# Products of identity and key lengths on VectorE, and the bonus sum behind the value products

## The chip, the cores and the metric

The kernel runs on one core of a Trainium2 chip. The metric is device time in microseconds from start to end of one execution of the program; the median over several executions is given. Engines are named as in the profile: PE is TensorE (matmuls; PEld its weight loads), DVE is VectorE, ACT is ScalarE, POOL is GpSimd, SP is SyncE, which issues most of the loads.

## The reference

One layer of a streaming encoder on x of 1 x 2048 x 1024 float32: a chunk-banded attention and an RWKV-7 recurrence side by side, a gated merge, and a feed-forward block. What matters here is the recurrence, with 8 heads of 64 channels:

```python
kk = heads(k * k_k)
kk = kk / jnp.maximum(jnp.sqrt(jnp.sum(kk * kk, axis=-1, keepdims=True)), 1e-12)
k = k * (1.0 + (a - 1.0) * k_a)
...
def step(state, inp):
    r_t, w_t, k_t, v_t, aa_t, bb_t = inp
    sa = jnp.einsum('bhij,bhj->bhi', state, aa_t)
    state = (state * w_t[:, :, None, :] + sa[..., None] * bb_t[:, :, None, :]
             + v_t[..., None] * k_t[:, :, None, :])
    y = jnp.einsum('bhij,bhj->bhi', state, r_t)
    return state, y

xs = tuple(jnp.moveaxis(t, 1, 0) for t in (r_h, w_h, k_h, v_h, -kk, kk * a_h))
...
bonus = jnp.sum(r_h * k_h * r_k.astype(jnp.float32), axis=-1, keepdims=True) * v_h
out = (yn + bonus) * heads(g)
```

## The kernel before

**Tiling and stages.** The 2048 positions are handled in four groups of 512 (`G`). For each group come the recurrence (`phase_rwkv`), the attention (`phase_attention`) and the merge (`phase_merge`); the feed-forward block follows for halves of the sequence. Dense products with the input weights run throughout: a float32 operand is split into a high and a low part, and three matmuls of 128x512 replace one (`mm3`, L83); ACT makes the high part of a weight block (L74), DVE the low one (L75).

**The recurrence.** A group has four pairs of heads, p = 0 to 3, handled as two batches of two; the first pair of a batch is the even one (p = 0 or 2), the second the odd one (p = 1 or 3). A group is cut into 8 chunks of 64 positions, and the recurrence inside a chunk is replaced by matrix products with the inverse of a triangular matrix. For each pair `rwkv_pre` makes everything that doesn't depend on the state: it mixes r, k and v (L353), computes decays (E, Ei), sums the squares of the keys (ps_ss, L441) and, on DVE, their reciprocals n2t (L443, L444); POOL spreads these with four small copies (L451) into n2, the key lengths by chunk and head of the pair (the profile leaves numbers out of names: n). Then come, in the order of the text:

- mN (L454), two products of 128x512, one for each head of the pair: the triangular mask mI, which holds for all chunks, times n2, both operands broadcast. Its only reader is L549, at the end of the preamble.
- AR and BK, scaled rows of keys and of r (L468 to L484).
- the bonus row: r times r_k times the key tk (L487, DVE), the sum over a head by a matmul with a block matrix of ones (ps_bonus, L489, PE), times v (L490, DVE), stored in `bvd[p]` by a DMA on POOL's queue (L491). `rwkv_post` reads it back (bv, L714) when the pair's recurrence is done.
- the value products: v times a centring matrix (ps_v, L498, PE), four ACT copies into SV (L502, L503).
- BK transposed on PE in two halves (ps_bk, L513), each multiplied by n2 on DVE into BR (L517).
- the products of BK and AR (ps_A, L533, PE), in two halves of two buffers each, and from these on DVE NA (L542), the rest of AR (L548) and the rest of BR (L549, with mN).

When both pairs of a batch are through, `rwkv_inverse` computes the triangular inverses of all their chunks in 31 steps of two small DVE instructions (L566, L572), with three block transpositions around them (L557, L575, L577); `rwkv_blocks` starts with matmuls of its result X1 (ps_t, L596). `rwkv_trans` and `rwkv_chunk` follow. Batch 1's preambles are interwoven with batch 0's recurrence: at each call of `between()` a list (`GATES`, `STEPS`) says how many gate products or recurrence steps stand at that place in the text.

**What sets the order.** Each engine works through one queue in a fixed order. The order is not that of the text: when the program is built, a scheduler plays it through with estimated durations, and each engine takes, of what is ready by that estimate, what stands first in the text. Dense matmuls of a later gate so fill places where PE would wait. On the chip the order stays as planned, and each instruction waits for its own inputs. Tiles of one tag share buffers in turn: all the PSUM results of the preamble (ps_ss, ps_bonus, ps_v, ps_bk, ps_A) and of the two following functions use tag `a` of pool `pa` with two buffers; mN has one buffer.

Of the kernel before, what the change touches and what calls it, by code (L numbers as in the profile page):

```python
# [8 lines left out]
F32 = mybir.dt.float32  # L9
# [3 lines left out]
ALU = mybir.AluOpType  # L13
# [4 lines left out]
P = 128  # L18
# [5 lines left out]
G = 512  # L24
GT = G // P
C = 64
NC = G // C
# [25 lines left out]
class Block:  # L53
# [342 lines left out]
    def rwkv_pre(self, g, p, rp, NA, between=lambda: None):  # L396
        nc = self.nc
# [3 lines left out]
        r = self.tmp("r")  # L401
# [12 lines left out]
        v = self.tmp("v")  # L414
# [31 lines left out]
        n2 = rp.tile([P, NC, 2], F32, tag="n2", name="n2")  # L446
        nc.gpsimd.memset(n2, 1.0)
        n2v = n2.rearrange("p (t h) e -> p h t e", h=2)
        for par in range(2):
            for h in range(2):  # L450
                nc.gpsimd.tensor_copy(n2v[par * C : par * C + C, h, :, par], n2t[h * C : h * C + C, :, par])  # L451
        mN = self.tp.tile([P, 2, NC, C], F32, tag="mN", bufs=1, name="mN")
        for par in range(2):
            nc.gpsimd.tensor_tensor(  # L454
                mN[:, par],
                self.mI[:, None, :].to_broadcast((P, NC, C)),
                n2[:, :, par, None].to_broadcast((P, NC, C)),
                ALU.mult,
            )
        between()  # L460

        AR = rp.tile([P, NC, 3, C], F32, tag="AR", name="AR")
# [22 lines left out]
        between()  # L485

        nc.vector.scalar_tensor_tensor(r, r, self.rk[:, col], tk, op0=ALU.mult, op1=ALU.mult)  # L487
        psb = self.pa.tile([P, G], F32, tag="a", name="ps_bonus")
        nc.tensor.matmul(psb, self.bones, r, start=True, stop=True)  # L489
        nc.vector.tensor_tensor(r, psb, v, ALU.mult)  # L490
        nc.gpsimd.dma_start(self.bvd[p], r)  # L491

        between()

        SV = rp.tile([P, NC, 2, C], F32, tag="SV", name="SV")
# [4 lines left out]
        for h in range(2):  # L500
            src = psv[h * C : h * C + C]
            nc.scalar.copy(SVv[C:P, h, :, 0], src[:, :, 0:C])  # L502
            nc.scalar.copy(SVv[0:C, h, :, 1], src[:, :, C:P])  # L503
        R["SV"] = SV

        between()

# [1087 lines left out]
```

## Time and profile before

| what | us |
|---|---|
| median of 3 runs | 3343.01 (3342.64 to 3346.67) |
| the profiled execution's own time | 3342.12 |
| its span in the profile | 3340.3 |

The granted clock of TensorE is 0.992 in the profiled execution. The DMA queues moved 478.42 MB, a mean of 143 GB/s. The span is what lies between the first and the last instruction that the profile shows; the execution's own time also holds what lies around it. In the profile's rows a group of instructions reads: line, engine, operation, written tile <- read tiles, partitions x elements, count | busy time, mean of one in ns | idle time of the engine just before them and what ended it. In a row of a timeline the first two numbers are start and duration in us, and the bracket at the end is the engine's idle time before it and its releaser. The waits view gives for each pair of waiter and releaser the total in us, how many times, and the longest.

The mix of the first low-rank columns (L352 on lw), with which a group's recurrence begins, starts at 35.0 us in the first group and at 1536.4 in the fourth; the last transpose of a post-processing (L704) starts at 1808.0.

### The profile page before, as it was taken

The numbers are of one execution on the slowest core, as the hardware profiler recorded it, in microseconds if no ns is written. First come the engines' busy times: TensorE is split into PE (matmuls) and PEld (weight loads), VectorE is DVE, ScalarE is ACT, GpSimd is POOL, SyncE is SP. The second block draws the span as 40 slices with busy tenths as digits, with TensorE's granted clock in tenths as the row PEclk, the third lists the DMA queues.
The fourth block names the chain that finished last, engine by engine and source line by source line (L and its number), as shares of the span: only waits on it lengthen the run. The fifth ranks groups of instructions, "written<-read, shape, count | busy, mean of one in ns | idle before, by whom it ended". The sixth has DMA issues, their size and how long they took to land. (4 is left out here: it accounts for less than half of the span.)

```text
span 3340.3 us, 49351 instructions
## 1 busy us (share of the span) xinstructions
PE 3247.1 (97%) x19089; PEld 2609.9 (78%) x19089; DVE 2282.6 (68%) x3806; ACT 1462.3 (44%) x2331; POOL 391.8 (12%) x732
## 2 busy tenths in 40 slices
PE   7999999999999999999999999999999999999998
PEld 6777787777778777777777777888888878888886
DVE  6774656765665775565774675876877777766778
ACT  4434634445644444644434644333331254554432
POOL 2210002111012110012210000111200011100002
PEclk9999999999999999999999999999999999999999
DMA  5224243125263225354224266434756364444443
GB/s 157 80 89 146 98 145 120 61 89 188 84 239 126 67 92 174 101 209 142 80 89 146 85 225 222 133 116 140 272 172 202 108 242 170 170 165 154 152 151 126
DMA packets 164945, 478.42 MB, mean 143 GB/s; under 512 B 17436, under 2 KB 34016, under 8 KB 162024
## 3 DMA queue, kind: packets, MB, share of 16 engines
q1 hardware_dynamic: 110004, 364.07, 32.8%
q0 software_dynamic: 18688, 63.98, 5.0%
q10 hardware_dynamic: 36020, 47.23, 3.9%
q8 instruction: 151, 2.47, 0.3%
q14 instruction: 82, 0.67, 0.1%
HBM read 355.64 MB, written 122.71 MB: 143 GB/s over the span
## 5 line engine op out<-in xcount | busy, mean ns | idle before, releaser
L83 PE MATMUL psd<-hh,whi 128*128 128x512 f32 x1344 | 542.6, 404 | 2.3 <-DVE QA L835 2.3
L83 PE MATMUL psd<-hl,whi 128*128 128x512 f32 x1344 | 539.4, 401 | 0.0
L83 PE MATMUL psd<-hh,wlo 128*128 128x512 f32 x1344 | 536.8, 399 | 0.0
L74 ACT CAST whi<-wraw 128x1024 fp32r<-128x1024 f32 x232 | 243.6, 1050 | 537.3 <-PE psd L83 423.7
L83 PE MATMUL ps_dn<-fop 128*128 128x512 f32 x1920 | 440.6, 391 | 3.0 <-DVE u L1291 2.4
L75 DVE TENSOR_TENSOR wlo<-wraw,whi 128x1024 fp32r<-128x1024 f32 x232 | 283.1, 1220 | 214.4 <-ACT whi L74 192.1
L83 PEld LDWEIGHTS ps_dn<-fop 128*128 128x128 f32 x1920 | 359.9, 188 | 79.5 <-DVE u L1291 3.4
L83 PEld LDWEIGHTS psd<-hh,whi 128*128 128x128 f32 x1344 | 256.1, 191 | 57.5 <-issue 3.4
L83 PEld LDWEIGHTS psd<-hh,wlo 128*128 128x128 f32 x1344 | 255.7, 190 | 54.0 <-issue 3.5
L83 PEld LDWEIGHTS psd<-hl,whi 128*128 128x128 f32 x1344 | 255.6, 190 | 50.9 <-issue 2.1
L83 PE MATMUL ps_dn<-fop,fop 128*128 128x512 f32 x1008 | 228.6, 389 | 0.0
L83 PEld LDWEIGHTS ps_dn<-fop,fop 128*128 128x128 f32 x1008 | 189.2, 188 | 39.3
L1291 DVE TENSOR_TENSOR u<-u,ps_dn 128x512 f32<-128x512 f32 x240 | 160.7, 683 | 54.9 <-PE ps_dn L83 54.4
L895 DVE CUSTOM_DVE_ANT_0 sc<-bias,ps_s 128x640 f32<-128x640 f32 (+4 forms) x128 | 94.1, 735 | 54.9 <-PE ps_s L889 44.0
L74 ACT CAST fop<-wdraw 128x1024 fp32r<-128x1024 f32 x40 | 41.9, 1047 | 192.0 <-DVE u L1291 88.7
L900 ACT ACTIVATE sc<-sc,mn 128x640 f32<-128x640 f32 (+4 forms) x128 | 97.8, 764 | 35.4 <-DVE mn L895 30.1
L74 ACT CAST s12h<-s 128x1024 fp32r<-128x1024 f32 x32 | 33.7, 1054 | 168.9 <-PE ps_u L83 168.8
L1019 PE MATMUL ps_o<-whi,mh 128*128 128x512 f32 x256 | 102.4, 400 | 2.2 <-ACT o L1025 2.2
L1019 PE MATMUL ps_o<-wlo,mh 128*128 128x512 f32 x256 | 102.5, 400 | 0.6 <-DVE wlo L75 0.6
L83 PE MATMUL ps_p<-yh,whi 128*128 128x512 f32 x256 | 102.2, 399 | 0.4 <-DVE th L985 0.4
L83 PE MATMUL ps_p<-yh,wlo 128*128 128x512 f32 x256 | 102.0, 398 | 0.0
L1019 PE MATMUL ps_o<-whi,ml 128*128 128x512 f32 x256 | 101.7, 397 | 0.0
(378 smaller groups left out, 6750.6 us busy)
## 6 DMA issues: line engine op xcount, KB each, us to landing
wraw<-in_w_in_dram SPq DMA_DIRECT2D x168, 512.0 KB, 3.6
wraw<-in_w_up_dram SPq DMA_DIRECT2D x80, 512.0 KB, 4.6
ar<-sd SPq DMA_DIRECT2D x21, 1024.0 KB, 4.8
wdraw<-in_w_down_dram SPq DMA_DIRECT2D x40, 512.0 KB, 4.2
araw<-ad SPq DMA_DIRECT2D x40, 512.0 KB, 4.4
gd<-gate ACTq DMA_DIRECT2D x64, 256.0 KB, 2.3
wraw<-in_w_out_dram SPq DMA_DIRECT2D x32, 512.0 KB, 3.6
ad<-r POOLq DMA_DIRECT2D x64, 256.0 KB, 2.4
```

The lines of the kernel that those rows point to most:

```text
L74: self.nc.scalar.copy(hi, src)
L75: self.nc.vector.tensor_tensor(lo, src, hi.bitcast(F32), ALU.subtract)
L83: mm = nc.tensor.matmul(ps, l, r, start=start and n == 0, stop=stop and n == last).ins
L895: nc.vector.tensor_tensor_reduce(sc[:, 0:n], bias[:, s0:640], pss[:, c0 : c0 + n], 1.0, 3.0e38, ALU.add, ALU.min, mn,)
L900: nc.scalar.activation(sc[:, 0:n], sc[:, 0:n], AF.Exp, scale=-1.0, bias=mn, accum_out=sm)
L1019: nc.tensor.matmul(ps[t], l[:, k, ts], r[:, k % 2], start=k == 0 and j == 0, stop=k == KB - 1 and j == 2)
L1291: nc.vector.tensor_tensor(u[t][:, ns], u[t][:, ns], ps, ALU.add)
```

## The change

Two blocks of `rwkv_pre` move. The two mN products leave POOL, where they stood behind the copies of n2, and stand on DVE behind the bonus row L487. The bonus matmul, its product with v and its DMA move behind the value products and the ACT copies, with the `between()` that stood after them now in front of the value products.

```diff
@@ -449,14 +449,6 @@
         for par in range(2):
             for h in range(2):
                 nc.gpsimd.tensor_copy(n2v[par * C : par * C + C, h, :, par], n2t[h * C : h * C + C, :, par])
-        mN = self.tp.tile([P, 2, NC, C], F32, tag="mN", bufs=1, name="mN")
-        for par in range(2):
-            nc.gpsimd.tensor_tensor(
-                mN[:, par],
-                self.mI[:, None, :].to_broadcast((P, NC, C)),
-                n2[:, :, par, None].to_broadcast((P, NC, C)),
-                ALU.mult,
-            )
         between()
 
         AR = rp.tile([P, NC, 3, C], F32, tag="AR", name="AR")
@@ -485,11 +477,14 @@
         between()
 
         nc.vector.scalar_tensor_tensor(r, r, self.rk[:, col], tk, op0=ALU.mult, op1=ALU.mult)
-        psb = self.pa.tile([P, G], F32, tag="a", name="ps_bonus")
-        nc.tensor.matmul(psb, self.bones, r, start=True, stop=True)
-        nc.vector.tensor_tensor(r, psb, v, ALU.mult)
-        nc.gpsimd.dma_start(self.bvd[p], r)
-
+        mN = self.tp.tile([P, 2, NC, C], F32, tag="mN", bufs=1, name="mN")
+        for par in range(2):
+            nc.vector.tensor_tensor(
+                mN[:, par],
+                self.mI[:, None, :].to_broadcast((P, NC, C)),
+                n2[:, :, par, None].to_broadcast((P, NC, C)),
+                ALU.mult,
+            )
         between()
 
         SV = rp.tile([P, NC, 2, C], F32, tag="SV", name="SV")
@@ -502,6 +497,11 @@
             nc.scalar.copy(SVv[C:P, h, :, 0], src[:, :, 0:C])
             nc.scalar.copy(SVv[0:C, h, :, 1], src[:, :, C:P])
         R["SV"] = SV
+
+        psb = self.pa.tile([P, G], F32, tag="a", name="ps_bonus")
+        nc.tensor.matmul(psb, self.bones, r, start=True, stop=True)
+        nc.vector.tensor_tensor(r, psb, v, ALU.mult)
+        nc.gpsimd.dma_start(self.bvd[p], r)
 
         between()
 
```

## The prediction

> **What bounds the kernel now.** I read the page first: its span and its busy times.
>
> ```profile
> span 3340.3 us, 49351 instructions
> ...
> PE 3247.1 (97%) x19089; PEld 2609.9 (78%) x19089; DVE 2282.6 (68%) x3806; ACT 1462.3 (44%) x2331; POOL 391.8 (12%) x732
> ```
>
> TensorE (PE) is busy in all but 3340.3 - 3247.1 = 93.2 us, so an edit that leaves its matmuls alone can only win or lose within its waits. Next the waits of PE, two rows of which touch the change:
>
> ```profile
> PE ps_t L596 <- DVE X L575: 26.6, 8, 3.8
> ...
> PE ps_bonus L489 <- DVE r L487: 8.1, 8, 1.2
> ```
>
> A preamble (rwkv_pre) runs 16 times, for pairs p = 0 to 3 in each of four groups. PE waits for the bonus row in 8 of them, and 8 times (two batches, four groups) for the end of the triangular inverse on VectorE. Together 34.7 us, over a third of all that PE idles. The order of time says which preambles. First pair 1 of the first group, from the timeline (columns: start, duration, engine, line, operation):
>
> ```profile
> 90.08 0.75 DVE L353 SCALAR_TENSOR_TENSOR v<-pr,cst,v 128x512 f32<-128x512 f32 x1
> ...
> 93.73 0.68 DVE L484 TENSOR_TENSOR BK<-tk,Ei 64x512 f32<-64x512 f32 x1
> 95.21 2.99 POOL L454 TENSOR_TENSOR mN<-mI,n 128x512 f32<-128x512 f32 x2
> 95.76 1.54 DVE L484 TENSOR_TENSOR BK<-tk,Ei 64x512 f32<-64x512 f32 x1
> 97.19 0.39 PE L83 MATMUL psd<-hh,whi 128*128 128x512 f32 x1
> 97.31 1.44 DVE L487 SCALAR_TENSOR_TENSOR r<-r,cst,tk 128x512 f32<-128x512 f32 x1
> 98.81 1.13 PE L489 MATMUL ps_bonus<-r,bones 128*128 128x512 f32 x2 [1.23 <-DVE r L487]
> ...
> 102.07 0.69 DVE L517 TENSOR_TENSOR BR<-ps_bk,n 128x512 f32<-128x512 f32 x1 [0.98 <-PE ps_bk L513]
> 103.11 0.69 DVE L517 TENSOR_TENSOR BR<-ps_bk,n 128x512 f32<-128x512 f32 x1 [0.36 <-PE ps_bk L513]
> 104.85 0.71 DVE L542 TENSOR_TENSOR NA<-ps_A,n 32x256 f32<-32x256 f32 x2 [1.04 <-PE ps_A L533]
> ...
> 143.85 1.20 PE L596 MATMUL ps_t<-X,NA 32*32 32x32 f32 x64 [2.83 <-DVE X L575]
> ```
>
> While GpSimd (POOL) makes the two products mN, the same L484 that took 0.68 us at 93.73 takes 1.54, and L487 takes 1.44 (a pair 0 row below shows 0.75). The stretch is 0.86 + 0.69 = 1.55 us, and PE waits 1.23 for r. That it is a habit and not an accident, the group rows say:
>
> ```profile
> L454 POOL TENSOR_TENSOR mN<-mI,n 128x512 f32<-128x512 f32 x32 | 43.9, 1388 | 1.3
> ...
> L484 DVE TENSOR_TENSOR BK<-tk,Ei 64x512 f32<-64x512 f32 x32 | 28.7, 896 | 0.0
> ...
> L487 DVE SCALAR_TENSOR_TENSOR r<-r,cst,tk 128x512 f32<-128x512 f32 x16 | 17.5, 1097 | 0.2
> ```
>
> (896 - 680) ns x 32 = 6.9 us and (1097 - 750) ns x 16 = 5.6 us, together 12.5: eight times 1.55. So the odd pairs (1 and 3) are stretched, the even ones not. After the bonus VectorE has hardly a gap up to the inverse's end; the stage view, taken between these moments, says so (columns: window, length, then busy time and count of PE, PEld, DVE, ACT, POOL):
>
> ```profile
> 105.00:144.00 39.00, 36.17 (x172) 29.20 (x173) 36.92 (x97) 16.18 (x24) 5.62 (x10) 1.00 0.27 85
> ...
> 206.50:245.00 38.50, 34.66 (x189) 27.77 (x188) 34.24 (x96) 13.64 (x20) 6.09 (x7) 1.00 0.33 117
> ```
>
> DVE is busy 36.92 of 39.00 us before pair 1's inverse ends and 34.24 of 38.50 before pair 3's. **So what bounds PE here is VectorE's path from the odd preamble to X (L575)**, not the bonus wait by itself. Pair 3 has the same shape:
>
> ```profile
> 197.06 1.54 DVE L484 TENSOR_TENSOR BK<-tk,Ei 64x512 f32<-64x512 f32 x1
> 198.62 1.44 DVE L487 SCALAR_TENSOR_TENSOR r<-r,cst,tk 128x512 f32<-128x512 f32 x1
> ...
> 200.12 1.12 PE L489 MATMUL ps_bonus<-r,bones 128*128 128x512 f32 x2 [0.80 <-DVE r L487]
> ...
> 203.47 0.52 DVE L679 SCALAR_TENSOR_TENSOR ST<-ps_st,gC,S 128x64 f32<-128x64 f32 x2 [0.91 <-PE ps_st L676]
> 204.25 0.69 DVE L517 TENSOR_TENSOR BR<-ps_bk,n 128x512 f32<-128x512 f32 x1 [0.26 <-PE ps_bk L513]
> ...
> 206.57 0.71 DVE L542 TENSOR_TENSOR NA<-ps_A,n 32x256 f32<-32x256 f32 x2 [0.65 <-PE ps_A L533]
> ...
> 244.93 1.83 PE L596 MATMUL ps_t<-X,NA 32*32 32x32 f32 x64 [3.84 <-DVE X L575]
> ```
>
> **The change, part by part.**
>
> *Products off GpSimd.* 32 instructions, 43.9 us of POOL, vanish. POOL is 12% busy and its own time is worth nothing; what counts is the 1.55 us of stretch in each odd preamble, 12.4 us in all, on VectorE's path to r and to X.
>
> *Products on VectorE.* The trace has no VectorE product of two stretched-out (broadcast) operands in SBUF. Neighbours:
>
> ```profile
> L1192 DVE TENSOR_TENSOR r<-r 128x512 f32<-128x512 f32 x64 | 43.8, 685 | 2.8 <-ACT r L1190 2.4
> ...
> L517 DVE TENSOR_TENSOR BR<-ps_bk,n 128x512 f32<-128x512 f32 x32 | 22.1, 690 | 15.4 <-PE ps_bk L513 15.1
> ...
> L421 DVE TENSOR_SCALAR tw<-tw 128x512 f32<-128x512 f32 x16 | 6.7, 421 | 0.0
> ```
>
> Same size and operation cost 685 to 690, one of them with the same key lengths n broadcast. The lower bound is 421 (one tensor input), the upper 1388, what GpSimd needs. I take 685: 1.37 us a preamble, 21.9 in all. In an odd preamble it lies on the path: 1.37 - 1.55 = -0.18. In an even one VectorE waits on others anyway:
>
> ```profile
> 59.66 0.75 DVE L487 SCALAR_TENSOR_TENSOR r<-r,cst,tk 128x512 f32<-128x512 f32 x1
> ...
> 63.15 0.69 DVE L517 TENSOR_TENSOR BR<-ps_bk,n 128x512 f32<-128x512 f32 x1 [0.82 <-PE ps_bk L513]
> 64.77 0.69 DVE L517 TENSOR_TENSOR BR<-ps_bk,n 128x512 f32<-128x512 f32 x1 [0.93 <-PE ps_bk L513]
> ...
> 92.72 2.41 POOL L451 COPY n<-n2t 64x4 f32<-64x4 f32 x4 [1.57 <-DVE n2t L444]
> ...
> 160.78 0.87 POOL L451 COPY n<-n2t 64x4 f32<-64x4 f32 x4 [8.94 <-DVE n2t L444]
> 162.22 0.69 DVE L662 TENSOR_TENSOR S<-ps_s,gC 128x512 f32<-128x512 f32 x1 [1.50 <-PE ps_s L661]
> ...
> 165.94 0.69 DVE L490 TENSOR_TENSOR r<-ps_bonus,v 128x512 f32<-128x512 f32 x1 [3.03 <-PE ps_bonus L489]
> ```
>
> Pair 0 has waits of 0.82 and 0.93 that cover 1.37, pair 2 has 1.50 and 3.03. Were that cover gone, each even preamble would cost up to 1.37, 11.0 us for eight.
>
> *The new wait.* VectorE's mN now needs n from POOL's four copies (L451). Behind mN on VectorE stand the bonus product (L490), the two L517 and, through their PSUM buffers, ps_bk and ps_A on PE. In pair 1 the copies end at 92.72 + 2.41 = 95.13, two microseconds before r could: no wait. In pair 2 they end at 161.65; 1.37 of products then end at 163.02 and S (L662), if it is queued behind them, starts 0.8 later than 162.22. PE's next transpose needs S's PSUM buffer, but has dense matmuls to put before it. Bounds 0 and 0.8 for each of four; I take 0.4, 1.6 us.
>
> *Bonus behind the value products.* Two matmul instructions, one VectorE product and one DMA on POOL's queue for each preamble are moved, none added. The value products need only v, which is ready 8 us before r (v's last step ended at 90.83, r at 98.75), so they can fill time in which PE had to wait, and the four ACT copies out of them no longer stand between bonus and second ps_bk. ps_bk now follows the bonus directly, and L490 and the two L517 can run back to back. The two buffers of the PSUM tag still alternate; the later bonus tile holds one until L490, which now sits behind 1.37 us of products. What the bonus DMA stores is read only in the post-processing of the pair, behind its whole recurrence, and on POOL's queue only memsets and small copies stand behind it: nothing.
>
> **The sum.** PE's order is drawn up at build time. It puts the bonus right behind the matmul at 97.19; unstretched, r would have ended at 95.76 + 0.68 + 0.75 = 97.19. So the plan knows nothing of the stretch, and PE's waits at bonus and inverse are what VectorE falls behind its plan. Pair 1: 1.23 + 2.83; pair 3: 0.80 + 3.84. Take away 1.55 of lateness and PE waits 1.55 less over the two places together, eight times: 12.4 us. The waits of VectorE inside the preamble (0.98 + 0.36 + 1.04 = 2.38 for pair 1, 0.91 + 0.26 + 0.65 = 1.82 for pair 3) are planned ones: if they go, VectorE is early, but the plan moves the inverse's matmuls forward by as much, and PE has no hole to fill there. So I count them only at the far end of the range. 12.4 - 1.6 = 10.8 us. The profiled execution took 3342.1 us; 3342.1 - 10.8 = 3331.3. The median of the runs shown is 3343.0, 0.9 above it: 3332 on that scale.
>
> **Rivals.**
>
> *The wait only moves (same).* If the new plan is no better kept than the old, VectorE's path shortens by only 0.18 an odd preamble, PE arrives 1.2 us earlier at pair 1's inverse (0.8 at pair 3's) and waits there instead: 8 x 0.18 = 1.4 us, 3341.6. For it: DVE's 36.92 of 39.00. Against it: the plan's error is the stretch itself, and that goes.
>
> *The regained waits count in full (faster).* With ps_bk, L490 and L517 back to back, VectorE's path loses the 2.38 and 1.82 us of waits too, and the plan's order of dense matmuls stays: 4 x (2.38 + 1.82) + 8 x 0.18 = 18.2, 3324.8. Against it: the sum's argument on the plan, and that some of the wait for ps_A stays, since PE must still work between the last L517 and L542.
>
> *Products ahead of their input (slower).* Place: VectorE's queue between the reciprocal of n2t and r, odd pairs. If the plan takes POOL's copies for short (0.87 at 160.78, against 2.41 at 92.72) and slots mN in ahead of the L484 of 93.73, VectorE stands until 95.13, 1.4 us, and the rest is late by it: 8 x (1.4 + 1.37 - 1.55) = 9.8 us, 3352.8. It decides only if VectorE comes to mN before 95.13, ahead of the last L484 (95.76). Against it: BK and r stand earlier in the program and their inputs are ready, so they go first.
>
> *A full VectorE gets more work (slower).* The even preambles' 11.0 us turn out not to be covered, since what VectorE does in them is pushed into the next stretch: 11.0 - 1.4 = +9.6, 3352.6. Against it stand the waits of pair 0 and 2 shown above. The Trainium skill, Perfetto Trace Analysis, section Optimizing Scalar/DVE Operations, speaks for this one: where VectorE is saturated, moving work to ScalarE or even GpSimd may help, so the reverse should hurt; it adds that moving between those two might not help. By the trace the first half holds for the two stretches alone, and the 1.55 us bear out the second.
>
> **How the numbers follow.** Forecast 0.50; wait only moves 0.28; full regain 0.08; products ahead of input 0.07; full VectorE 0.07. A measurement of this kernel tells about 0.2%, 6.7 us, from no change. Forecast and full regain are beyond it: faster 0.58; the moved wait is within it: same 0.28; the last two are slower: 0.14. The range leaves out those two and reaches from 2 us under the full regain past the moved wait to a part of a late input: 3323 to 3346. The bounds of the product's price (421 to 1388) move an odd preamble by -0.5 to +1.4, which the two ends and the slower rivals span. The forecast alone would span 3327 to 3336.
>
> **What would show it.** Right: L484 and L487 have means near 680 and 750 ns; mN stands on DVE at about 685, 32 times; the PE row ps_bonus <- r falls from 8.1 to under 2 us; the sum of the two PE rows falls from 34.7 by 10 or more. Moved wait: the bonus row goes but ps_t <- X rises by 6 or more. Ahead of its input: a wait of mN on POOL's n. Full VectorE: ps_t <- X well above 34. I would be wrong if the new order opens holes elsewhere, such as in the attention stage, that these rows don't show.

## The result

| kernel | median us (runs) | profiled execution us | its span us | granted clock |
|---|---|---|---|---|
| before | 3344.36 (3341.08 to 3347.52, 19) | 3342.12 | 3340.3 | 0.992 |
| changed | 3352.47 (3344.48 to 3355.41, 19) | 3353.25 | 3351.5 | 0.990 |

The changed kernel takes 1.0022 of the time before, interval 1.0015 to 1.0028: slower by 0.2%, some 8 us, where 10.8 us less were forecast.

### The profile after

First the page: its span and busy times.

```profile
span 3351.5 us, 49356 instructions
...
PE 3253.0 (97%) x19089; PEld 2615.1 (78%) x19089; DVE 2290.0 (68%) x3838; ACT 1462.5 (44%) x2331; POOL 341.7 (10%) x700
```

PE idles 3351.5 - 3253.0 = 98.5 us (93.2 before), and it is also busy 5.9 us longer with the same 19089 matmuls. Then the groups by line that the prediction named; L476 and L479 are the old L484 and L487, and mN stands on L482.

```profile
L476 DVE TENSOR_TENSOR BK<-tk,Ei 64x512 f32<-64x512 f32 x32 | 21.8, 682 | 0.0
...
L482 DVE TENSOR_TENSOR mN<-mI,n 128x512 f32<-128x512 f32 x32 | 21.0, 687 | 3.4 <-POOL n L451 3.4
...
L479 DVE SCALAR_TENSOR_TENSOR r<-r,cst,tk 128x512 f32<-128x512 f32 x16 | 12.0, 752 | 0.2
```

The same view for PE:

```profile
L502 PE MATMUL ps_bonus<-r,bones 128*128 128x512 f32 x32 | 17.3, 621 | 0.0
...
L596 PE MATMUL ps_t<-X,NA 32*32 32x32 f32 x512 | 13.9, 225 | 31.8 <-DVE X L575 31.8
```

The stretch is gone (682 and 752 ns), the products cost 687 ns as priced, and PE no longer waits for the bonus row. But its wait for X, 26.6 us before, is 31.8. In order of time, in the first group (rows of PE from the timeline):

```profile
138.73 1.20 PE L596 MATMUL ps_t<-X,NA 32*32 32x32 f32 x64 [3.00 <-DVE X L575]
...
141.55 0.63 PE L83 MATMUL psd<-hh,whi 128*128 128x512 f32 x1
141.97 0.63 PE L83 MATMUL psd<-hl,whi 128*128 128x512 f32 x1
...
144.33 0.40 PE L83 MATMUL psd<-hl,whi 128*128 128x512 f32 x1
144.56 0.40 PE L83 MATMUL psd<-hh,wlo 128*128 128x512 f32 x1
...
245.73 1.92 PE L596 MATMUL ps_t<-X,NA 32*32 32x32 f32 x64 [4.96 <-DVE X L575]
```

Two things are to be seen. Batch 1's wait (at 245.73) has grown from 3.84 to 4.96, past the 3.84 + 0.80 that PE waited there and at pair 3's bonus before. And behind a wait one dense matmul follows the other after 0.42 us (141.55 to 141.97), a little later after 0.23 (144.33 to 144.56): for a while TensorE ran at half clock, as the clock's record says too (half from 140.65 to 144.06).

How the recurrences stand as a whole is read from the stage view, each group's window taken from the first lw mix to the first QA of the attention (window, length, then busy times of PE, PEld, DVE, ACT, POOL, then the granted clock). First and last row of before, with the sum over the four groups:

```profile
34.95:310.36 275.41, 265.24 (x2195) 211.51 (x2194) 179.87 (x379) 117.34 (x203) 49.26 (x77) 0.99 0.32 105
...
1536.44:1813.30 276.86, 266.80 (x2199) 213.37 (x2198) 180.26 (x379) 118.34 (x203) 50.87 (x82) 0.98 0.29 94
sum 1105.38, PE 1064.93 PEld 850.99 DVE 720.68 ACT 472.36 POOL 201.09; mean PE 266.23 PEld 212.75 DVE 180.17 ACT 118.09 POOL 50.27
```

and the same of the changed kernel:

```profile
33.91:310.01 276.10, 266.39 (x2195) 213.05 (x2194) 181.72 (x387) 117.39 (x202) 36.45 (x69) 0.98 0.33 105
...
1543.88:1822.07 278.19, 268.54 (x2199) 215.16 (x2198) 182.24 (x387) 118.37 (x204) 37.92 (x74) 0.98 0.29 95
sum 1111.06, PE 1072.21 PEld 858.26 DVE 728.45 ACT 472.51 POOL 150.31; mean PE 268.05 PEld 214.56 DVE 182.11 ACT 118.13 POOL 37.58
```

The four recurrences became 5.7 us longer: PE's idle time in them fell by only 1.6 (1105.38 - 1064.93 = 40.5, 1111.06 - 1072.21 = 38.9), and its busy time rose by 7.3. The rest of the span's 11.2 us, 5.5, lies outside, in stages whose code is the same in both (last section but one).

### What the two traces say of the two batches

**Batch 0.** X came 4.1 us earlier: ps_t starts at 138.73 - 33.91 = 104.82 us from the group's start, against 143.85 - 34.95 = 108.90. That is more than the 1.55 of the stretch, since the waits of VectorE inside the preamble went too. But PE was there earlier as well: of the group's dense matmuls (psd) 388 now stand ahead of ps_t in PE's order, 400 before, counted in the traces. Twelve at 0.23 us are 2.8. So PE's two waits of 1.23 + 2.83 became one of 3.00.

**Batch 1.** ps_t starts 1.8 us *later* (245.73 - 33.91 = 211.82, against 244.93 - 34.95 = 209.98), though batch 0 ended 4.1 earlier. The 2.8 us of dense work that batch 0 was let off stand here. And VectorE's order at the join of the batches has turned round. Before (rows of DVE and POOL; var and yn belong to batch 0's post-processing, N and T to batch 1's inverse):

```profile
213.09 0.67 DVE L692 TENSOR_REDUCE var<-yq 128x8 f32<-128x512 f32 x1
...
214.13 1.67 POOL L695 TENSOR_TENSOR grs<-var,nhalf 128x8 f32<-128x8 f32 x1
...
214.24 2.04 DVE L557 STREAM_TRANSPOSE N<-NA 128x1024 f32<-128x1024 f32 x1
...
216.19 0.66 DVE L697 TENSOR_TENSOR yn<-ps_y,grs 128x512 f32<-128x512 f32 x1
...
220.62 0.69 DVE L697 TENSOR_TENSOR yn<-ps_y,grs 128x512 f32<-128x512 f32 x1 [1.82 <-POOL grs L695]
```

GpSimd's power grs takes 1.67 us, and the transposition N, standing between var and yn, hides it for the first of the two yn; the second waits 1.82. In the changed kernel (rows of DVE) N has slipped ahead of var:

```profile
212.31 1.97 DVE L557 STREAM_TRANSPOSE N<-NA 128x1024 f32<-128x1024 f32 x1
...
214.56 0.67 DVE L692 TENSOR_REDUCE var<-yq 128x8 f32<-128x512 f32 x1
...
218.33 0.69 DVE L697 TENSOR_TENSOR yn<-ps_y,grs 128x512 f32<-128x512 f32 x1 [1.85 <-POOL grs L695]
...
221.66 0.69 DVE L697 TENSOR_TENSOR yn<-ps_y,grs 128x512 f32<-128x512 f32 x1 [1.68 <-POOL grs L695]
```

Now VectorE stands for both powers, with the whole inverse behind it. The group rows say that it is so in every group: 12 waits became 16 (before, then changed).

```profile
L697 DVE TENSOR_TENSOR yn<-ps_y,grs 128x512 f32<-128x512 f32 x16 | 10.9, 682 | 23.7 <-POOL grs L695 23.7
```

```profile
L697 DVE TENSOR_TENSOR yn<-ps_y,grs 128x512 f32<-128x512 f32 x16 | 11.1, 692 | 30.6 <-POOL grs L695 30.6
```

**PE's longer busy time.** Two parts of the 7.3 us are seen. In the four recurrences the recorded clock was at half for 34.1 us before and for 51.2 after. Of that, 31.2 and 40.5 fall on time in which PE was busy, so some (40.5 - 31.2) / 2 = 4.7 more were lost to it. And the products ps_A take longer (before, then changed):

```profile
L533 PE MATMUL ps_A<-AR,BK 64*128 64x128 f32 x512 | 63.3, 285 | 2.6 <-DVE BR L549 2.6
```

```profile
L533 PE MATMUL ps_A<-AR,BK 64*128 64x128 f32 x512 | 68.1, 284 | 2.6 <-DVE BR L549 2.6
```

It is the odd pairs: there the small matmuls are broken up oftener by dense ones, and the 32 of a preamble hold PE for 4.34 us in the first group's pairs 1 and 3, 3.88 and 3.85 before. The two parts are more than 7.3 together. Taken from each matmul's start to the next one's, ps_A holds PE for 4.2 us more and ps_v for 1.0 more, ps_bk and ps_bonus for 1.4 and 1.1 less; with the 4.7 that makes 7.4.

### The profile page after: what moved, and what is told of

The parts are those of the page before. It is cut to its first block, busy times and chain, and to the rows that moved or that the text cites. A ratio compares the mean times of both kernels' runs of the same rounds, so it can differ in the third digit from the quotient of the medians.

```text
span 3351.5 us, 49356 instructions
## 1 busy us (share of the span) xinstructions
PE 3253.0 (97%) x19089; PEld 2615.1 (78%) x19089; DVE 2290.0 (68%) x3838; ACT 1462.5 (44%) x2331; POOL 341.7 (10%) x700
```

## The experiments

The expectations speak of these theories. **A**: PE's wait for VectorE's inverse decides, the plan fixes where ps_t stands, and a long wait brings half clock behind it. **B**: the 21 us more work on a full VectorE are the loss. **C**: the new place of the bonus sum is what costs. **G** came later: the loss comes from the power grs, which came into the open at batch 1. Ratios are to the kernel before, run on the same chip beside them, five rounds each.

### One edit alone

e1 is the changed kernel with the bonus block back where it stood (the diff is against the changed kernel); e2 the kernel before with the bonus block moved as in the change.

```diff
+        psb = self.pa.tile([P, G], F32, tag="a", name="ps_bonus")
+        nc.tensor.matmul(psb, self.bones, r, start=True, stop=True)
+        nc.vector.tensor_tensor(r, psb, v, ALU.mult)
+        nc.gpsimd.dma_start(self.bvd[p], r)
+
         mN = self.tp.tile([P, 2, NC, C], F32, tag="mN", bufs=1, name="mN")
...
         R["SV"] = SV
-
-        psb = self.pa.tile([P, G], F32, tag="a", name="ps_bonus")
-        nc.tensor.matmul(psb, self.bones, r, start=True, stop=True)
-        nc.vector.tensor_tensor(r, psb, v, ALU.mult)
-        nc.gpsimd.dma_start(self.bvd[p], r)
```

> Only the engine changes: mN on VectorE behind the bonus row, the bonus matmul, its product and its DMA stay ahead of the value products as in the kernel before. Theory A (PE waits for VectorE's inverse, the plan sets where in PE's order that wait falls, and each wait of about 3 us or more is followed by TensorE at half clock): the stretch of BK and r is gone, so the bonus wait goes (8.1 to under 1.5 us), and since the plan here leaves as many dense matmuls ahead of the inverse's products as before in batch 0 (401 against 399) and 11 more in batch 1, the waits for X fall from 26.6 to about 20 us: 3326 to 3338 us. Theory B (21 us more work on a full VectorE is the loss): as slow as the change, 3350 to 3354. Theory C (the loss is the bonus' new place): no slower than before, 3336 to 3345.

> Only the place changes: mN stays on GpSimd where it was, the bonus follows the value products. Theory A: the stretch of BK and r stays, and the plan puts the inverse's products 14 dense matmuls (3.2 us) earlier in batch 0 and 1 earlier in batch 1, so bonus and X waits together are 36 us or more and the half clock comes more often: 3350 to 3362 us. Theory B: no more VectorE work, so as before, 3341 to 3347. Theory C: as slow as the change, 3350 to 3355.

e1: 3343.71 us, 0.9998 (0.9989 to 1.0007). e2: 3348.53 us, 1.0005 (0.9996 to 1.0014). Neither part alone costs or brings anything that can be told. For e1 that refutes B (it has all of the new work on VectorE), misses A's gain and lies where C put it; e2, where A and C asked for 3350 us or more, has no loss that can be told. So the loss comes only when the bonus sum moves on top of the products: from e1 to the changed kernel the ratio goes from 0.9998 to 1.0022, and the intervals lie apart. Of e1's page:

```profile
span 3342.0 us, 49365 instructions
...
PE 3245.2 (97%) x19089; PEld 2607.2 (78%) x19089; DVE 2288.8 (68%) x3838; ACT 1462.3 (44%) x2331; POOL 350.7 (10%) x700
```

PE is busy 7.8 us less than in the changed kernel (3245.2 against 3253.0) and idles 1.7 less (96.8 against 98.5). Two sizes are known: half clock on a busy PE in the recurrences, 32.2 us against 40.5, some 4.1 lost, and ps_A, 3.6.

e1 shows the forecast at work in batch 0 and lost in batch 1: X came 1.4 to 1.6 us earlier, PE's waits there fell from 4.06 to 2.71, but batch 1's rose from 4.64 to 5.28, with 16 waits for grs as in the changed kernel. The wait of PE for X, all groups:

```profile
PE ps_t L596 <- DVE X L575: 31.9, 8, 5.3
```

In e2 the waits for grs stay at 23.2 us, 12 times: the turn of VectorE's order comes with the products. PE's earlier arrival comes with the bonus sum: ahead of the two ps_t of a group stand 400 and 606 dense matmuls before, 402 and 617 in e1, 386 and 605 in e2, 388 and 606 in the changed kernel. ps_A is at 64.5 us in e1, 1.2 above before; its 68.1 come only with both edits.

### Dense work ahead of the inverse's products

e3 and e4 change only what stands ahead of ps_t in PE's order: the r mix of pair 3 (24 dense matmuls) is written ahead of batch 0's first step, and one gate product more ahead of batch 1's. In phase_rwkv, with rwkv_pre calling early() ahead of its first between() and mixing r only where it isn't given:

```diff
-            nxt = [self.rwkv_pre(g, 2 + q, rp, NA, between) for q in range(2)]
+            r3 = []
+            def early():
+                r3.append(self.tmp("r"))
+                self.mix(g, 3, r3[0])
+            nxt = [self.rwkv_pre(g, 2, rp, NA, between, early=early)]
+            nxt.append(self.rwkv_pre(g, 3, rp, NA, between, r=r3[0]))
...
-            gate()
+            gate(2)
             rec = rec_of(NA, nxt, 1)
```

> The changed kernel with dense products written ahead of the inverse's products: pair 3's r mix is written ahead of the first recurrence step of batch 0, and one gate more ahead of batch 1's recurrence, so that PE's order has 20 and 18 dense matmuls (4.5 and 4.1 us) more ahead of ps_t. Theory A: the waits for X fall from 31.8 to about 4 us (4 times 0.9) and the half clock in the recurrences goes: 3305 to 3320 us. Theory B: VectorE is the bound, so PE waits as long at another place: 3342 to 3354.

> The kernel before with the same two moves: 8 and 18 dense matmuls (1.8 and 4.1 us) more ahead of ps_t. Theory A: the waits for X fall from 26.6 to about 4 us (4 times 1.0), the bonus waits of 8.1 us stay, and the half clock goes: 3308 to 3322 us, and within 6 us of the changed kernel with the same moves. Theory B: without the 21 us of products on VectorE it is 8 us or more faster than the changed kernel with the same moves.

e3: 3337.24 us, 0.9976 (0.9966 to 0.9985). e4: 3338.21 us, 0.9979 (0.9971 to 0.9988). Both fell short of what was expected, and they are alike, which speaks against B a second time. With 408 dense matmuls ahead of it batch 0's ps_t waits no more in e3, though a new wait of 1.76 for Z, which ACT makes, stands behind it, and the loss of the change is made up. Batch 1's still waits 3.66 a group: 18 dense matmuls more stand ahead of it (624 against 606, some 4.1 us), but PE also comes there earlier, since it lost less at batch 0.

A gate product more ahead of batch 1 (gate(3) for gate(2)): e5 does it to the changed kernel, e6 to e1, e8 to the kernel before, each with the early mix of e3.

> The changed kernel with the r mix of pair 3 ahead of batch 0's first step, as in e3_after_hold, and three gate products instead of two ahead of batch 1's inverse products: those then have 648 dense matmuls ahead of them in PE's order, against 624 in e3_after_hold and 606 in the changed kernel. Theory A (what is left to win is PE's wait at batch 1's inverse, 3.66 us a group in e3, and the half-clock stretch of 3.41 us that follows it, some 1.7 us lost): 24 matmuls more are 5.4 us, the wait goes, and 4 x (3.7 + 1.7) = 21 us fall from 3337: about 3316 to 3324, ps_t<-X under 2 us. Rival (the dense work is then missing at the end of batch 1's recurrence, which waits for its steps instead): the wait of ps_t goes but PE waits as much in ps_st, ps_tq or ps_yt, 3335 to 3340.

> Only the products on VectorE (bonus sum ahead of the value products as before), with the same holds as e5_after_hold3. Theory A (with no wait of PE at the inverses the bonus' place costs and brings nothing): within 3 us of e5_after_hold3. Theory C (the bonus' new place costs by itself, 4 to 8 us, where it isn't hidden by waits): 4 to 8 us faster than e5_after_hold3. The wait for the bonus row stays gone.

> The kernel before with the same holds as e5_after_hold3 (408 and 648 dense matmuls ahead of ps_t). It tells what the whole change is worth where PE doesn't wait for the inverses. Theory A: the wait for the bonus row stays (8 us), ps_t<-X goes, 3320 to 3328, 2 to 8 us above e5_after_hold3. Theory B (21 us of work more on VectorE is what costs): e8 faster than e5_after_hold3 by 5 us or more.

e5: 3350.07 us, 1.0017 (1.0008 to 1.0026). e6: 3348.77 us, 1.0005 (0.9996 to 1.0015). e8: 3346.88 us, 1.0002 (0.9993 to 1.0010). The rival held in kind, but in another place, and e5 and e8 came out slower than any range given for them. The three intervals overlap, so B and C can't be told apart here. In e5 ps_t<-X is off the list of waits, and these are new on it:

```profile
PE ps_s L898 <- DMA KK<-kc: 9.1, 3, 3.4
...
PE ps_g L83 <- DVE yn L699: 6.0, 4, 1.5
```

As the rows read, the gates are used up sooner, batch 1's post-processing has nothing to hide behind, and the attention waits for its keys. Here filling a wait with work from later on paid only as long as there was work to spare.

### The power out of the open

e7 is the changed kernel, e9 the kernel before, with one edit: batch 0's two yn stand behind the fourth step of batch 1's inverse on VectorE.

```diff
         nc.gpsimd.tensor_tensor(rs, var, self.nhalf, ALU.pow)
+        yield
         yn = self.tmp("yn").rearrange("p (c t) -> p c t", t=C)
-        nc.vector.tensor_tensor(yn, Y, rs[:, :, None].to_broadcast((P, NC, C)), ALU.mult)
+        with self.tc.issue_after(self.step):
+            nc.vector.tensor_tensor(yn, Y, rs[:, :, None].to_broadcast((P, NC, C)), ALU.mult)
...
-            for _ in range(3):
-                advance(inv, 8)
+            advance(inv, 4)
+            for p in post:
+                advance(p, 1)
+            for n in (4, 8, 8):
+                advance(inv, n)
                 gate()
```

`self.step` is the inverse's last X instruction so far (L572). The post-processing of batch 1 has the same new stop and is led past it by advance(p, 2) where it had advance(p, 1).

> The changed kernel with one difference: the two products yn of batch 0's post-processing stand behind the fourth step of batch 1's inverse on VectorE, not ahead of its second, so that VectorE doesn't stand waiting for GpSimd's power grs. PE's order keeps 388 and 605 dense matmuls ahead of the two ps_t. Theory (batch 1's X is late by the second wait for grs, 1.7 to 1.9 us, that came in with the products on VectorE): yn<-grs falls from 30.6 to under 16 us, ps_t of batch 1 waits 1.5 to 3 us less a group (4.96 to some 2.5), half-clock stretches become fewer, 3340 to 3346 where the changed kernel takes 3352. Rival (VectorE is late for other reasons and the idle time only moves): ps_t of batch 1 still waits 4.5 to 5, 3350 to 3354.

> The kernel before with e7_yn_later's edit alone (the two products yn behind the fourth step of batch 1's inverse). Before has one exposed wait for grs there (1.82 us a group), the changed kernel two (1.85 + 1.68). Theory G (the change lost at batch 1 because VectorE's order let the second grs come into the open; take both out and what the change wins on VectorE is seen): e9 gains less on its kernel than e7_yn_later did on the changed one (16 us): 4 x 1.8 = 7 us and a few half-clock stretches, 3336 to 3341, ps_t<-X about 20, the bonus row stays at 8. Rival (the yn edit is worth the same everywhere and the change stays 8 us slower beside it): 3326 to 3331.

e7: 3336.27 us, 0.9973 (0.9964 to 0.9982), against 1.0022 for the changed kernel: 16 us for an edit that adds and removes no work. Its rows (waits, and VectorE's timeline):

```profile
PE ps_t L596 <- DVE X L575: 21.5, 8, 3.0
...
DVE yn L699 <- POOL grs L695: 16.5, 8, 2.1
```

```profile
218.56 0.22 DVE L572 TENSOR_TENSOR X<-X,T 128x56 f32<-128x56 f32 x1
218.69 1.28 DVE L699 TENSOR_TENSOR yn<-ps_y,grs 128x512 f32<-128x512 f32 x2
```

VectorE takes both yn without a wait, having made four inverse steps meanwhile; the eight waits left are those of batch 1's own post-processing. Batch 1's ps_t waits 2.8 to 2.9 in two groups and 1.8 to 1.9 in the other two, instead of 4.9 to 5.0. So the exposed power was what made batch 1 late. Not all was as expected: e7 beat its range (3340 to 3346), and e9, 3334.59 us, 0.9966 (0.9954 to 0.9978), lies between G's range and the rival's: its one exposed wait was worth 11 us, not 7. The rival's other half, a change that stays 8 us slower, did not come about. With the power hidden on both sides the change is worth nothing that can be told (0.9973 and 0.9966, intervals overlapping), rather than 8 us of loss.

### Both sets of moves

e10 is the changed kernel, e11 e1, e12 the kernel before, each with the moves of e3 and of e7.

> The changed kernel with both, e7_yn_later's order of yn and e3_after_hold's moves (the r mix of pair 3 early, two gate products ahead of batch 1's inverse products; 408 and 624 dense matmuls ahead of ps_t). Theory A with G (PE's wait at batch 1's inverse was 3.66 in e3; X comes some 3.5 us earlier without the waits for grs): ps_t<-X under 3 us in all, the half-clock stretch after it goes, 4 x (3.5 + 1.7) = 21 us less than e3's 3337: 3318 to 3326. Rival (the work is missing in the tail then, as in e5_after_hold3): 3330 to 3337.

> The same with the products on VectorE alone (the bonus sum ahead of the value products, as before). Theory A: within 3 us of e10_after_yn_hold. Theory C (the bonus sum's new place costs by itself): 4 to 8 us faster than e10.

> The kernel before with both, yn's order and the holds. With waits for the inverse gone in both, e10 and e12 differ by the change's own parts: the wait for the bonus row (8 us) against 21 us more work on VectorE. Theory A: 4 to 10 us slower than e10. Theory B (VectorE's work is the loss): faster than e10 by 4 us or more. Neither: within 3 us, so that the change is worth nothing once VectorE is not late.

e10: 3327.00 us, 0.9938 (0.9925 to 0.9952). e11: 3322.91 us, 0.9935 (0.9922 to 0.9948). e12: 3337.22 us, 0.9970 (0.9961 to 0.9980). Here the change pays: (0.9970 - 0.9938) x 3345.55 us, the median of before beside them, are 10.7 us, and the intervals lie apart. e10 and e11 beat both kernels. e11 is 4.1 us faster than e10 by the medians, as C asked, but only 0.0003 by the ratios, and the intervals overlap: the bonus sum's place can't be told here. e10 misses its own range by 1 us, and ps_t<-X, forecast under 3 us, is 8.3. The waits of PE in e10 and the sum row of the stage view over its recurrences, then the same of e12:

```profile
PE ps_t L605 <- ACT Z L600: 8.4, 6, 1.7
PE ps_t L598 <- DVE X L577: 8.3, 4, 2.5
```

```profile
sum 1085.96, PE 1064.98 PEld 851.77 DVE 726.86 ACT 473.87 POOL 160.55; mean PE 266.25 PEld 212.94 DVE 181.71 ACT 118.47 POOL 40.14
```

```profile
PE ps_t L605 <- ACT Z L600: 15.0, 8, 2.0
...
PE ps_bonus L491 <- DVE r L489: 8.6, 8, 1.2
...
PE ps_t L598 <- DVE X L577: 5.4, 7, 1.0
```

```profile
sum 1099.79, PE 1064.86 PEld 850.51 DVE 721.17 ACT 474.27 POOL 197.30; mean PE 266.22 PEld 212.63 DVE 180.29 ACT 118.57 POOL 49.32
```

PE is busy as long in both (1065.0 and 1064.9), and idles 13.9 us less in e10 (1085.96 - 1064.98 = 21.0 against 1099.79 - 1064.86 = 34.9): the bonus row's 8.6 are gone and stay gone, and the two rows of ps_t fell from 20.4 to 16.7. The power is not wholly hidden in e10, though (waits of VectorE, e10, then e12; and GpSimd's timeline in e10):

```profile
DVE yn L701 <- POOL grs L697: 21.7, 12, 2.1
```

```profile
DVE yn L701 <- POOL grs L697: 16.4, 8, 2.1
```

```profile
215.93 3.12 POOL L697 TENSOR_TENSOR grs<-var,nhalf 128x8 f32<-128x8 f32 x1
```

The first power of a group takes 3.12 us there instead of 1.67, with a VectorE product wlo of 1.20 us beside it, and the second yn of batch 0 waits 1.32. What is left of ps_t<-X in e10 stands at batch 1 alone, behind this wait; no run shows what the change brings without it.

The settings together, ratios to before:

| | before's order of parts | the change |
|---|---|---|
| as they are | 1 | 1.0022 |
| dense work ahead of ps_t | 0.9979 | 0.9976 |
| one gate more | 1.0002 | 1.0017 |
| yn put later | 0.9966 | 0.9973 |
| dense work ahead of ps_t and yn put later | 0.9970 | 0.9938 |

## Why the prediction was wrong

**What bounds the kernel.** Right, as far as it went: moves in order alone, which add and remove no work, took the kernel before from 1 to 0.9966 and the changed kernel from 1.0022 to 0.9938. It read batch 1's path from odd preamble to X by its busy share alone and did not list what else stands on it; the post-processing of batch 0, with GpSimd's power in it, does.

**Products off GpSimd, products on VectorE.** Right: 682 and 752 ns against the 680 and 750 named, 687 against 685. Even preambles and added work cost nothing that shows (e1; e10 against e12).

**The new wait on n.** Right in its place, pair 2 of each group and no other, but 0.85 us there (two waits, 0.5 at the longest), where 0.4 was taken and 0.8 was the bound: 3.4 us of VectorE over all instead of 1.6.

**The bonus sum's move.** Priced at nothing, and alone it is worth nothing (e2). On top of the products it costs 0.24% (e1 against the changed kernel): PE stands at ps_t 14 dense matmuls earlier in batch 0 (402 to 388) and 11 in batch 1 (617 to 606), half clock takes more, and ps_A takes 3.6 us of PE more by its group row. Nothing in the prediction looked at how the plan would place ps_t or break up other matmuls.

**The sum: the step that failed.** It said that PE's order is drawn up at build time, that PE's waits are what VectorE falls behind that plan, and: "Take away 1.55 of lateness and PE waits 1.55 less over the two places together, eight times". This holds for a fixed plan. The changed program got a new plan, and in it each engine's order shifted. For batch 0 it came out near all the same: VectorE won 4.1, the plan took 2.8 by moving ps_t ahead of twelve dense matmuls, and PE's waits went from 4.06 to 3.00, 1.06 less instead of 1.55. For batch 1 the sign was wrong: 4.64 became 4.96, since the power came into the open there. To it comes a new wait of 0.56 in batch 0's recurrence steps (ps_st<-ST, at 189.4 us in the first group), which isn't the power's, since it stands ahead of it and e7 has it too; e1 doesn't. Over four groups 4 x 1.06 - 4 x 0.88 = 0.7 us less waiting instead of 10.8, and on top of it half clock and ps_A made PE busy for longer. e7 shows that the power is what made batch 1 late. It isn't what parts the changed kernel from e1, which has the same 16 waits for it and takes the time of before; that step is the bonus sum's. e10 against e12 shows that with the power less in the way and dense work ahead the change does bring a gain. That its 10.7 us lie so near to 10.8 is luck: by its rows it is the bonus wait and the wait for Z (6.6 less), while ps_t<-X is 2.9 more in e10.

**The rivals.** The moved wait named the right row: the bonus row went and ps_t<-X rose, by 5.2 us where "6 or more" was asked. It gave 3341.6, since it left VectorE's path to X unhurt. The full VectorE's 3352.6 met the measured time, but not by its mechanism: e1 has the same work there at the time of before. Products ahead of their input did not come about: in the odd pairs mN waited for nothing. "The new order opens holes elsewhere" was named as what would make the forecast wrong; it was given no price and no place, and it should have been the slower rival, at the first GpSimd result that VectorE waits for with the inverse behind it.

**Still open.** Of the 11.2 us between the two spans 5.5 lie outside the recurrences: 3.8 more from the third group's attention to the end of its merge, where PE waited 2.1 for th, 2.5 more in the feed-forward block, and 1.0 less ahead of the first recurrence. e1 has the same 5.6 outside at the time of before, and over the kernels without the third gate this part varies from 2234.9 (before, the shortest) to 2244.2 us (e3) with the code unchanged, so nothing of the loss is laid to it or denied to it. Why ps_A is broken up oftener only with both edits, and how the bonus sum's cost divides between half clock, ps_A and the rest, wasn't tried.

## What to carry to other kernels

Where the order of each engine is planned at build time, as here, an edit that makes one engine faster can give a new order to all of them: before adding up what is won, list every wait that is now hidden on the path from the edit to the place where it should pay, and ask what happens when neighbours there change places. A slow result of another engine (here a power of 128x8 on GpSimd, 1.67 us) that VectorE waits for with a long serial chain behind it is best placed by hand a few steps down that chain. Judge an edit that shortens a path once more with the next obstacle taken away: the same edit was worth +0.2% here, nothing, and -0.3%, by what stood behind it.

## What the runs showed of the hardware

**The clock behind a wait.** TensorE's clock drops to half behind waits, in stretches of 3.41 us or two or three times that. Three windows behind ps_t, before's two and the changed kernel's second (the third number from the end is the granted clock):

```profile
143.80:148.00 4.20, 4.15 (x78) 3.34 (x78) 4.16 (x7) 3.96 (x7) 0.00 (x0) 1.00 0.27 106
244.90:250.30 5.40, 5.37 (x73) 4.51 (x73) 1.68 (x2) 3.39 (x6) 0.00 (x0) 0.52 0.26 97
```

```profile
245.70:252.40 6.70, 6.67 (x132) 5.47 (x133) 1.66 (x2) 3.62 (x6) 0.00 (x0) 0.69 0.26 78
```

Over the 14 profiles of this case, between 30 and 3320 us, half clock set in within 7.5 us from the start of PE's waits in this way:

| PE's wait, us | waits | followed by half clock |
|---|---|---|
| 4 to 5.5 | 12 | 12 |
| 2.75 to 4 | 36 | 34 |
| 1.8 to 2.75 | 53 | 33 |
| 1.3 to 1.8 | 86 | 30 |
| 0.8 to 1.3 | 193 | 3 |

So a wait of 3 us mostly costs, by estimate, at least 1.7 us more behind it (half of 3.41), and by this table two waits of 1.2 us that lie apart cost less than one of 2.4. Close together it may differ: in e5 and e6 half clock came four times behind two waits of 0.7 and 0.5 us within 1.6 us of each other. That was read off the profiles; no kernel was made for it alone. The Trainium skill, TensorE: Matmul & The Clock Gate, Part 1 (The HAM clock gate), gives a free-running window of 3413 ns, and its section Why this matters for your kernels asks for no idle gaps of TensorE over some 3 us. The trace agrees with the window, since the stretches are 3.41 us or whole multiples; the gap that is safe here was nearer to 1.3 us than to 3. The prediction left this cost out.

**GpSimd beside VectorE.** The stretch that the prediction read out of before went both ways: with the two mN products away, VectorE's 64x512 products BK fell from a mean of 896 ns to 682, and in the changed kernel GpSimd's small var (L693, at 215.32 us), 0.19 us alone, took 1.22 where VectorE made wlo beside it (1.21 us from 215.27). In e10 the power grs took 3.12 us instead of 1.67 beside wlo.
